# Feed-forward entry on Trainium2: seven of eight sums of quarters of the normalised rows on GpSimd instead of VectorE

## The chip, the cores and the metric

The kernel runs on one core of a Trainium2 chip. A core has TensorE (matrix products and transposes, results in PSUM), VectorE, ScalarE and GpSimd (elementwise work, each with an instruction queue of its own that it executes in order) and SyncE, which here issues all DMAs. The metric is the device time of one execution in microseconds (us). Before the change it was 2821.42 us, the median of three runs (2820.86 to 2824.37).

## The reference

A trunk of two layers over 512 tokens of width 1024. Each layer has four sublayers, each between two RMS norms and added to the running state `h`: a feed-forward block, a mixer (a gated delta rule in the first layer, a state-space scan in the second), a cross attention over 256 memory rows, and another feed-forward block. So there are four feed-forward blocks, and they are what the change touches:

```python
def swiglu(x, w_in, w_out):
    gate, up = jnp.split(x @ w_in, 2, axis=-1)
    return (jax.nn.silu(gate) * up) @ w_out

u = swiglu(rms_norm(h, g[0, 0]), ffn_w_in[l, 0], ffn_w_out[l, 0])
h = h + MACARON_W * rms_norm(u, g[0, 1])
```

`x` is 512 x 1024, `w_in` 1024 x 5632, `w_out` 2816 x 1024, all in float32.

## The kernel before

Every float32 product is made of three products in a reduced format: each operand is split into a high part (a cast, by ScalarE) and a low part (the difference, by VectorE), and high x high, high x low and low x high are added up in PSUM (`mm3`, L144 to L146).

The feed-forward block computes gate and up with a scheme after Strassen and Winograd: the 512 x 1024 input is cut in four quarters, A11 and A21 being the left half of the columns of tokens 0 to 255 and 256 to 511, A12 and A22 the right half. Seven products of quarters and of sums of quarters replace eight. The sums needed are S1 = A21 + A22, S2 = S1 - A11, S3 = A11 - A21 and S4 = A12 - S2.

The tokens come in four tiles of 128. `FFN.enter(i, ss, tag)` (L367) takes tile i of the state, normalises it on VectorE (L374, two halves of 512 columns: `u <- h, rcol, pg`), and for each quarter or sum calls `put`: four transposes on TensorE into one PSUM bank (L380), the high part by ScalarE (L382), the low part by VectorE (L383). Tiles 0 and 1 give A11 and A12. Tiles 2 and 3 ("third" and "fourth") give A22, S1, S2, S4 and S3; the sums are formed with the rows of tile i - 2, in place, by four instructions of 128 x 512: s1 (L392), S3's operand (L394), S2's operand (L395), S4's operand (L397). Each but the second needs the one before it or s1, and S2's operand needs s1, S4's operand needs S2's.

Entry is not a stage of its own. `run` calls for each tile i the last output products of the sublayer before (`tail`), then `post` (the norm behind that sublayer, L226 and L231 on VectorE), then `enter`. With the fourth tile `head(0)` begins: the weights of the first two pairs are loaded and split (L130, L131), and products of A11 and A12 alone are formed (`early`), which need nothing of tiles 2 and 3. After that comes `plain`, which forms a difference of raw weights (L455) and splits it (`split`, L138 and L139), and later `pair` (L474).

The order of the instructions on each engine is not written by hand: a scheduler places them by priority (`later` shifts it) and by its own estimate of how long each takes. So a change of engine for one instruction moves others, too. PSUM tiles `ps_c` (the transposes) have two banks, the tile `xs` (s1) two buffers.

Of the kernel before, what the change touches and what calls it, by code (L numbers as in the profile page):

```python
# [14 lines left out]
ALU = mybir.AluOpType  # L15
# [38 lines left out]
def prio(name):  # L54
    def wrap(f):
        def g(self, *a, **k):
            with getattr(self, "t", self).later(name):
                return f(self, *a, **k)
        return g
    return wrap  # L60
# [275 lines left out]
class FFN:  # L336
# [29 lines left out]
    @prio('ff_enter')  # L366
    def enter(self, i, ss, tag):  # L367

        t, nc = self.t, self.t.nc
        r = t.rcol(ss)  # L370
        x = t.u[:, i, :]
        a, b = slice(0, T), slice(T, D)
        for s in (a, b):
            nc.vector.scalar_tensor_tensor(x[:, s], t.h[:, i, s], r[:, 0:1], self.pg[:, s], op0=ALU.mult, op1=ALU.mult)  # L374
        ts = slice(i % 2 * P, i % 2 * P + P)

        def put(src, dst):
            ps = t.bank(tag)
            for k in range(4):
                nc.tensor.transpose(ps[:, k * P:k * P + P], src[:, k * P:k * P + P], t.cst(C_ID))  # L380
            p = ps.rearrange("p (k t) -> p k t", k=4)
            nc.scalar.copy(dst[0][:, :, ts], p)  # L382
            nc.vector.tensor_sub(dst[1][:, :, ts], p, dst[0][:, :, ts])  # L383

        if i < 2:
            put(x[:, a], self.A11)
            put(x[:, b], self.A12)
        else:
            y = t.u[:, i - 2, :]
            put(x[:, b], self.A22)  # L390
            s1 = t.nt.tile([P, T], F32, name="xs", bufs=2)
            nc.vector.tensor_add(s1, x[:, a], x[:, b])  # L392
            put(s1, self.S1)
            nc.vector.tensor_sub(x[:, a], y[:, a], x[:, a])  # L394
            nc.vector.tensor_sub(y[:, a], s1, y[:, a])  # L395
            put(y[:, a], self.S2)
            nc.vector.tensor_sub(y[:, b], y[:, b], y[:, a])  # L397
            put(y[:, b], self.S4)
            put(x[:, a], self.S3)

# [921 lines left out]
def run(t, phases, n0=0):  # L1322
# [17 lines left out]
    with ExitStack() as c:  # L1340
        if hasattr(phases[0], "gains"):
            phases[0].gains(c, n0)
            phases[0].sums()
        for i in range(NT):
            if i:
                t.load(i)
            ss = t.nt.tile([P, 2], F32, name="ssh", bufs=2)
            for f in range(2):
                t.sumsq(t.h[:, i, f * T:f * T + T], ss[:, f:f + 1], f and i < 2)
            enter(i, n0, phases[0], ss, "cscc"[i])  # L1350
            if i % 2:
                phases[0].head(i // 2, i == 1)
        t.load_rest()
    for j, ph in enumerate(phases):
        n = n0 + j
        nxt = phases[j + 1] if j + 1 < len(phases) else None
        with ExitStack() as c:
            if hasattr(nxt, "gains"):
                nxt.gains(c, n + 1)
            ph.open(c)  # L1360
            t.post_gain(n)
            t.warm(AF.Silu, t.xh[:, KB - 1, T - 1:T])
            ph.rest()
            if hasattr(nxt, "sums"):
                nxt.sums()
            for i in range(NT):
                t.tail(ph, i)
                if i == 0:
                    t.warm(AF.Sqrt, t.ssu[:, 0, 0:1])
                if i == NT - 1:  # L1370
                    c.close()
                    if nxt:
                        nxt.head(0)
                ss = t.post(i, nxt)
                if nxt:
                    enter(i, n + 1, nxt, ss)
                else:
                    for f in range(2):
                        fs = slice(f * T, f * T + T)
                        nc.sync.dma_start(out=t.ap["out"][i * P:(i + 1) * P, fs], in_=t.h[:, i, fs])  # L1380
            if nxt:
                nxt.head(1)
# [41 lines left out]
```

## Time and profile before

| | |
|---|---|
| median of three runs | 2821.42 us |
| the profiled execution | 2822.96 us |
| its span | 2821.2 us |
| TensorE busy | 2771.5 us (98%) |
| VectorE busy | 2078.6 us (74%) |
| ScalarE busy | 1509.3 us (53%) |
| GpSimd busy | 129.4 us (5%) |
| mean granted TensorE clock | 0.998 |

The span is the time from the first to the last instruction of the profiled execution; that execution was 1.54 us longer than the median. Shares are means over the whole span. In the rows below DVE is VectorE, ACT ScalarE, POOL GpSimd, PE TensorE; "L392" is line 392 of the kernel. A row of the timeline has the start, the time taken, the engine, the line, the operation, output<-inputs, the count, and in brackets how long the engine had been idle before and for what it had waited.

### The profile page before, as it was taken

How to read it: one execution, taken by the hardware profiler on the slowest of the kernel's cores; microseconds unless marked ns; L12 is line 12 of the kernel's file. 1: busy time of each engine (PE TensorE's matmuls, PEld its weight loads, DVE VectorE, ACT ScalarE, POOL GpSimd, SP SyncE). 2: the span in 40 equal slices, each digit the busy share in tenths (PEclk: the TensorE clock that was granted, in tenths of full speed). 3: DMA queues.
4: the chain of work that ended last, by engine and by line, in shares of the span. 5: the costliest groups of instructions: out<-in, count | busy, mean ns of one | idle time of the engine just before them, and what ended most of it. 6: DMA issues, size and time to landing. Idle time of an engine off the chain costs nothing.

```text
span 2821.2 us, 45001 instructions
## 1 busy us (share of the span) xinstructions
PE 2771.5 (98%) x17328; PEld 2451.3 (87%) x17328; DVE 2078.6 (74%) x4057; ACT 1509.3 (53%) x2760; POOL 129.4 (5%) x141
## 2 busy tenths in 40 slices
PE   8999999999999999999999999999999999999998
PEld 7999987888887887999988999888888888799997
DVE  8887777767667565887778877777667766588776
ACT  5444486766475574544355444575554656454433
POOL 0000001100000000000000000013212200000000
PEclk9999999999999999999999999999999999999999
DMA  6333534233324532332343332433233363133233
GB/s 217 106 105 103 159 124 119 77 115 86 100 71 138 189 113 79 121 113 90 112 150 128 98 105 96 147 121 112 83 105 110 100 223 112 69 112 113 96 107 105
DMA packets 144758, 326.51 MB, mean 116 GB/s; under 512 B 36080, under 2 KB 65520, under 8 KB 144032
## 3 DMA queue, kind: packets, MB, share of 16 engines
q1 hardware_dynamic: 144544, 323.63, 35.3%
q8 instruction: 137, 2.24, 0.3%
q14 instruction: 77, 0.63, 0.1%
HBM read 297.27 MB, written 26.31 MB: 115 GB/s over the span
## 4 chain that ended last, share of the span: by engine, by line
PE 84%; DVE 7%; ACT 4%; DMA 3%; issue 1%; POOL 0%; SPq 0%; DVEq 0%; ACTq 0%; POOLq 0%
PE ps_a L144 16%; PE ps_a L145 16%; PE ps_a L146 16%; PE ps_s L145 5%; PE ps_s L146 4%; PE ps_s L144 4%; PE ps_c L144 2%; PE ps_c L146 2%; PE ps_c L145 2%; PE ps_f L145 2%; PE ps_f L146 2%; PE ps_f L144 2%; DVE wlo L131 1%; PE ps_c L1060 1%; PE ps_s L1229 1%
## 5 line engine op out<-in xcount | busy, mean ns | idle before, releaser
L144 PE MATMUL ps_a<-xh,whi 128*128 128x256 f32 (+1 forms) x2368 | 751.7, 320 | 2.8 <-ACT z L871 1.6
L145 PE MATMUL ps_a<-xl,whi 128*128 128x256 f32 (+1 forms) x2368 | 748.9, 318 | 0.3 <-DVE xl L383 0.3
L146 PE MATMUL ps_a<-xh,wlo 128*128 128x256 f32 (+1 forms) x2368 | 746.4, 317 | 0.0
L144 PEld LDWEIGHTS ps_a<-xh,whi 128*128 128x128 f32 x2368 | 452.0, 191 | 31.6 <-ACT xh L382 2.0
L145 PEld LDWEIGHTS ps_a<-xl,whi 128*128 128x128 f32 x2368 | 452.9, 191 | 26.6 <-DVE xl L383 0.7
L146 PEld LDWEIGHTS ps_a<-xh,wlo 128*128 128x128 f32 x2368 | 452.9, 191 | 23.9
L131 DVE TENSOR_TENSOR wlo<-raw,whi 128x1024 fp32r<-128x1024 f32 x278 | 340.7, 1228 | 172.6 <-ACT whi L130 170.6
L130 ACT CAST whi<-raw 128x1024 fp32r<-128x1024 f32 x278 | 289.6, 1043 | 219.6 <-PE ps_a L145 122.8
L138 ACT CAST whi<-h 128x1024 fp32r<-128x1024 f32 x168 | 175.6, 1048 | 203.2 <-PE ps_a L145 149.8
L139 DVE TENSOR_TENSOR wlo<-h,whi 128x1024 fp32r<-128x1024 f32 x168 | 205.3, 1224 | 89.1 <-ACT whi L138 88.5
L493 ACT CAST bh<-raw 128x512 fp32r<-128x512 f32 x80 | 49.7, 621 | 167.6 <-DMA raw<-ffn_in 135.7
L145 PE MATMUL ps_s<-wlo,hhi 128*128 128x512 f32 x352 | 138.0, 392 | 0.0
L144 PE MATMUL ps_s<-whi,hhi 128*128 128x512 f32 x352 | 137.8, 392 | 0.0
L146 PE MATMUL ps_s<-whi,hlo 128*128 128x512 f32 x352 | 137.2, 390 | 0.0
L146 PE MATMUL ps_c<-whi,hlo 128*128 128x512 f32 x288 | 112.0, 389 | 0.0
L144 PE MATMUL ps_c<-whi,hhi 128*128 128x512 f32 x288 | 112.0, 389 | 0.0
L145 PE MATMUL ps_c<-wlo,hhi 128*128 128x512 f32 x288 | 112.0, 389 | 0.0
L138 ACT CAST whi<-raw 128x1024 fp32r<-128x1024 f32 x80 | 84.0, 1050 | 51.0 <-PE ps_c L146 39.4
L486 DVE TENSOR_TENSOR h<-raw 128x512 f32<-128x512 f32 x80 | 55.1, 689 | 70.7 <-DMA raw<-ffn_in 67.5
L139 DVE TENSOR_TENSOR wlo<-raw,whi 128x1024 fp32r<-128x1024 f32 x80 | 97.5, 1219 | 9.0 <-ACT whi L138 9.0
L513 ACT ACTIVATE h<-h 128x512 f32<-128x512 f32 x80 | 50.6, 633 | 83.8 <-DVE h L510 83.6
L469 ACT CAST hhi<-h 128x512 fp32r<-128x512 f32 x88 | 54.8, 622 | 72.1 <-DVE h L514 43.1
(418 smaller groups left out, 6620.3 us busy)
## 6 DMA issues: line engine op xcount, KB each, us to landing
raw<-ffn_in SPq DMA_DIRECT2D x192, 512.0 KB, 4.2
raw<-ffn_out SPq DMA_DIRECT2D x88, 512.0 KB, 3.5
raw<-dn_in SPq DMA_DIRECT2D x48, 512.0 KB, 3.5
raw<-ssd_in SPq DMA_DIRECT2D x32, 512.0 KB, 3.6
hd<-h SPq DMA_DIRECT2D x24, 512.0 KB, 3.2
h<-hd SPq DMA_DIRECT2D x24, 512.0 KB, 4.3
raw<-dn_out SPq DMA_DIRECT2D x16, 512.0 KB, 3.8
raw<-xa_k SPq DMA_DIRECT2D x16, 512.0 KB, 4.3
```

The source lines that it names most:

```text
L130: nc.scalar.copy(hi[:, :n], raw[:, :n])
L131: nc.vector.tensor_sub(lo[:, :n], raw[:, :n], hi[:, :n])
L138: nc.scalar.copy(hi, raw)
L139: nc.vector.tensor_sub(lo, raw, hi)
L144: mm(ps, lhs[0], rhs[0], start=first, stop=False)
L145: mm(ps, lhs[0], rhs[1], start=False, stop=False)
L146: mm(ps, lhs[1], rhs[0], start=False, stop=last)
L469: self.t.nc.scalar.copy(hi, x)
L486: sub(T1, u[:, a], g[:, a])
L493: nc.scalar.copy(b22[0], u[:, b])
L513: nc.scalar.activation(gt, gt, AF.Silu)
L1060: nc.tensor.matmul(py[:, e * 64:e * 64 + 64], st["gp"][e][:, c, :], st["xt"][:, c, e * 64:e * 64 + 64], start=True, stop=True)
```

## The change

In `enter`, for the third tile all four sums are formed by GpSimd, for the fourth tile the last three; the first sum of the fourth tile (s1) stays on VectorE. That is seven instructions in each of the four entries. Nothing else is edited; what is computed is the same.

```diff
             put(x[:, b], self.A22)
             s1 = t.nt.tile([P, T], F32, name="xs", bufs=2)
-            nc.vector.tensor_add(s1, x[:, a], x[:, b])
+            op = nc.gpsimd.tensor_tensor
+            if i == 2:
+                op(s1, x[:, a], x[:, b], op=ALU.add)
+            else:
+                nc.vector.tensor_add(s1, x[:, a], x[:, b])
             put(s1, self.S1)
-            nc.vector.tensor_sub(x[:, a], y[:, a], x[:, a])
-            nc.vector.tensor_sub(y[:, a], s1, y[:, a])
+            op(x[:, a], y[:, a], x[:, a], op=ALU.subtract)
+            op(y[:, a], s1, y[:, a], op=ALU.subtract)
             put(y[:, a], self.S2)
-            nc.vector.tensor_sub(y[:, b], y[:, b], y[:, a])
+            op(y[:, b], y[:, b], y[:, a], op=ALU.subtract)
             put(y[:, b], self.S4)
             put(x[:, a], self.S3)
```

Lines behind the edit have numbers that are higher by four in the changed kernel (L455 is L459, for example).

TensorE in the fourth entry, third tile, before: from the transposes of A22 (`u`) and of S1 (`xs`) on; behind the last row shown 14 more products stand before the transposes of S2.

```order
L380 MATMUL ps_c<-const,u 128x128 [waits DVE_49,PE_49]
L380 MATMUL ps_c<-const,u 128x128 x3
L144 MATMUL ps_s<-thi,xh 128x512
L380 MATMUL ps_c<-const,xs 128x128 [waits DVE_49,PE_49]
L380 MATMUL ps_c<-const,xs 128x128 x3
L145 MATMUL ps_s<-tlo,xh 128x512
```

The same place in the changed kernel, down to the transposes of S2 (the last `u`).

```order
L380 MATMUL ps_c<-const,u 128x128 [waits DVE_49,PE_49]
L380 MATMUL ps_c<-const,u 128x128 x3
L144 MATMUL ps_s<-thi,xh 128x512
L380 MATMUL ps_c<-const,xs 128x128 [waits PE_49,Pool_49]
L380 MATMUL ps_c<-const,xs 128x128 x3
L145 MATMUL ps_s<-tlo,xh 128x512
L146 MATMUL ps_s<-thi,xl 128x512
L144 MATMUL ps_a<-xh,whi 128x256
L145 MATMUL ps_a<-xl,whi 128x256
L146 MATMUL ps_a<-xh,wlo 128x256
L380 MATMUL ps_c<-const,u 128x128 [waits DVE_49,Pool_49]
```

Five products stand between the transposes of S1 and those of S2 where there were 15, and both now wait for GpSimd (Pool).

VectorE at the same place before, from the second half of L374 of the third tile to its low part of S2.

```order
L374 SCALAR_TENSOR_TENSOR u<-h,rcol,pg 128x512
L392 TENSOR_TENSOR xs<-u 128x512 [waits DVE_49]
L455 TENSOR_TENSOR h<-raw 128x512 [waits DMAHW0_49]
L394 TENSOR_TENSOR u<-u 128x512 [waits DVE_49]
L383 TENSOR_TENSOR xl<-ps_c,xh 128x4x128 [waits Activation_49]
L395 TENSOR_TENSOR u<-xs,u 128x512 [waits DVE_49]
L383 TENSOR_TENSOR xl<-ps_c,xh 128x4x128 [waits Activation_49]
L397 TENSOR_TENSOR u<-u 128x512 [waits DVE_49]
L226 TENSOR_TENSOR u<-u,gbc 128x512 [waits Activation_49]
L383 TENSOR_TENSOR s2l<-ps_c,s2h 128x4x128 [waits Activation_49]
```

And in the changed kernel, down to the low part of S3.

```order
L374 SCALAR_TENSOR_TENSOR u<-h,rcol,pg 128x512
L459 TENSOR_TENSOR h<-raw 128x512 [waits DMAHW0_49]
L383 TENSOR_TENSOR xl<-ps_c,xh 128x4x128 [waits Activation_49]
L139 TENSOR_TENSOR wlo<-h,whi 128x1024 [waits Activation_49]
L383 TENSOR_TENSOR xl<-ps_c,xh 128x4x128 [waits Activation_49]
L383 TENSOR_TENSOR s2l<-ps_c,s2h 128x4x128 [waits Activation_49]
L226 TENSOR_TENSOR u<-u,gbc 128x512 [waits Activation_49]
L203 TENSOR_TENSOR rcol<-ssu 128x1
L383 TENSOR_TENSOR s4l<-ps_c,s4h 128x4x128 [waits Activation_49]
L459 TENSOR_TENSOR h<-raw 128x512 [waits DMAHW1_49,DVE_49]
L383 TENSOR_TENSOR s3l<-ps_c,s3h 128x4x128 [waits Activation_49]
```

The four sums are gone from VectorE's queue, the split L139 has moved ahead of the low part of S1, and the low parts of S2, S4 and S3 stand ahead of the norm of the next tile (L231, three rows further on) as before.

TensorE in the third entry, third tile, in the changed kernel: the transposes of S1 follow those of A22 directly, where six products stood between them.

```order
L380 MATMUL ps_c<-const,u 128x128 [waits DVE_49,PE_49]
L380 MATMUL ps_c<-const,u 128x128 x3
L380 MATMUL ps_c<-const,xs 128x128 [waits PE_49,Pool_49]
L380 MATMUL ps_c<-const,xs 128x128 x3
L145 MATMUL ps_a<-xl,whi 128x256
```

Behind them 17 products follow before the transposes of S2, where there were 22.

## Rows read from the trace of the kernel before

**Rows 1.** Busy time, share and instructions by engine, from the page.

```profile
PE 2771.5 (98%) x17328; PEld 2451.3 (87%) x17328; DVE 2078.6 (74%) x4057; ACT 1509.3 (53%) x2760; POOL 129.4 (5%) x141
```

**Rows 2.** Waits of PE: who for whom, us in total, times, longest.

```profile
PE ps_c L380 <- DVE u L374: 13.5, 8, 7.8
```

**Rows 3.** Windows: busy per engine, PEclk, DMA share and GB/s, third entry.

```profile
1490.00:1495.00 5.00, 1.62 (x14) 1.43 (x13) 4.97 (x10) 1.84 (x6) 0.00 (x0) 1.00 0.68 246
...
1496.20:1503.00 6.80, 5.70 (x27) 5.17 (x27) 5.02 (x9) 3.91 (x8) 0.00 (x0) 0.52 0.16 60
```

**Rows 4.** One moved line's durations (min/median/max), and the group of L1044.

```profile
L394 DVE TENSOR_TENSOR u<-u x8: 678/688/692, 24.4 to 2476.3; 128x512 f32<-128x512 f32 x8
...
L1044 POOL TENSOR_TENSOR gp<-gp,di 128x512 f32<-128x512 f32 x32 | 47.2, 1475 | 123.1 <-DVE gp L1040 97.6 <-DVE rsy L313 13.1 <-ACT sjunk L1104 6.2
```

**Rows 5.** Timeline of GpSimd, 1899 to 1905 us.

```profile
1899.53 1.29 POOL L1044 TENSOR_TENSOR gp<-gp,di 128x512 f32<-128x512 f32 x1 [17.51 <-DVE gp L1040]
1900.91 0.60 POOL L1043 TENSOR_SCALAR di<-const,rows 128x128 f32<-128x128 f32 x1
1901.48 3.71 POOL L1044 TENSOR_TENSOR gp<-gp,di 128x512 f32<-128x512 f32 x1
```

**Rows 6.** Timeline of VectorE beside it.

```profile
1901.34 2.70 DVE L1036 SCALAR_TENSOR_TENSOR gp<-gp,sA,const 128x128 f32<-128x128 f32 x10
```

**Rows 7.** Timeline of VectorE: alone, beside GpSimd with PSUM, beside GpSimd with SBUF.

```profile
1929.85 1.22 DVE L1100 TENSOR_TENSOR y<-y,sz 128x1024 f32<-128x1024 f32 x1
...
1945.69 0.73 DVE L1117 SCALAR_TENSOR_TENSOR solo<-ps_c,sng,sohi 128x512 fp32r<-128x512 f32 x1
...
1967.13 1.94 DVE L1100 TENSOR_TENSOR y<-y,sz 128x1024 f32<-128x1024 f32 x1
```

**Rows 8.** Timeline of GpSimd at the second and third of these.

```profile
1945.62 1.29 POOL L1044 TENSOR_TENSOR gp<-gp,di 128x512 f32<-128x512 f32 x1
...
1966.70 1.28 POOL L1044 TENSOR_TENSOR gp<-gp,di 128x512 f32<-128x512 f32 x1 [4.41 <-DVE gp L1040]
```

**Rows 9.** Timeline of VectorE, fourth entry.

```profile
2459.95 1.40 DVE L374 SCALAR_TENSOR_TENSOR u<-h,rcol,pg 128x512 f32<-128x512 f32 x2
...
2462.99 0.69 DVE L455 TENSOR_TENSOR h<-raw 128x512 f32<-128x512 f32 x1 [0.91 <-DMA raw<-ffn_in]
...
2470.57 1.40 DVE L231 SCALAR_TENSOR_TENSOR h<-u,rcol,h 128x512 f32<-128x512 f32 x2
...
2474.16 1.42 DVE L374 SCALAR_TENSOR_TENSOR u<-h,rcol,pg 128x512 f32<-128x512 f32 x2
```

**Rows 10.** Timeline of TensorE, fourth entry: S1 of tile three, S3 of tile four.

```profile
2462.23 0.63 PE L380 MATMUL ps_c<-const,xs 128*128 128x128 f32 x4
...
2480.89 0.60 PE L380 MATMUL ps_c<-const,u 128*128 128x128 f32 x4
```

**Rows 11.** Timeline of ScalarE, fourth entry: the cast of the raw difference.

```profile
2463.72 1.05 ACT L138 CAST whi<-h 128x1024 fp32r<-128x1024 f32 x1 [0.96 <-DVE h L455]
```

**Rows 12.** Timeline of VectorE, second entry.

```profile
1125.01 0.69 DVE L455 TENSOR_TENSOR h<-raw 128x512 f32<-128x512 f32 x1
```

**Rows 13.** Timeline of VectorE, third entry.

```profile
1479.82 1.40 DVE L374 SCALAR_TENSOR_TENSOR u<-h,rcol,pg 128x512 f32<-128x512 f32 x2
1481.15 0.68 DVE L226 TENSOR_TENSOR u<-u,gbc 128x512 f32<-128x512 f32 x1
...
1485.42 1.21 DVE L131 TENSOR_TENSOR wlo<-raw,whi 128x1024 fp32r<-128x1024 f32 x1
```

**Rows 14.** Timeline of TensorE, third entry: A22 and S3 of tile four.

```profile
1495.01 0.63 PE L380 MATMUL ps_c<-const,u 128*128 128x128 f32 x4 [3.40 <-DVE u L374]
...
1502.98 0.60 PE L380 MATMUL ps_c<-const,u 128*128 128x128 f32 x4
```

**Rows 15.** Timeline of VectorE, first entry.

```profile
20.98 1.22 DVE L131 TENSOR_TENSOR wlo<-raw,whi 128x1024 fp32r<-128x1024 f32 x1
```

## The prediction

> **What bounds the kernel now.** I read the busy shares first: TensorE is busy for 98% of the span [rows 1]. So a saving elsewhere counts only where TensorE stands still, and a new stop of TensorE counts in full. The list of who waited for whom comes second: TensorE's largest wait is that of the transposes (L380) for the normalised rows (L374), 13.5 us in eight places, 7.8 us of it in one, at the start, where the first rows have to be loaded [rows 2]. The places are the feed-forward entries, of which there are four: at about 10 to 40, 1105 to 1150, 1465 to 1505 and 2440 to 2487 us. Third, the windows around the third entry: TensorE is busy for 1.62 of 5 us there, and behind that gap its granted clock averages 0.52 over 6.8 us, which is the lower of its levels, 1.2 GHz instead of 2.4 [rows 3]. That stretch loses (1 - 0.52) x 6.8 = 3.3 us. Fourth, the timelines of VectorE, GpSimd and TensorE inside the entries, from which the terms come.
>
> **What is moved.** Each entry forms four sums per tile (S1's operand s1, then those of S3, S2, S4) for the third and the fourth tile. Seven of the eight go from VectorE to GpSimd: 28 instructions in all. On VectorE one took 0.69 us [rows 4]. No plain add or subtraction of this shape runs on GpSimd before; the nearest is the addition at L1044, 128x512 in float32, 1.475 us on the mean [rows 4] and 1.29 us when nothing holds it, with the next GpSimd instruction 1.38 us behind its start [rows 5]. I take 1.29 us and 1.38 us from step to step. The low bound is VectorE's own 0.69, the high one the 3.71 us below.
>
> **What the two engines do to each other.** The second L1044 in rows 5 took 3.71 us. Beside it VectorE ran ten instructions in a row with two operands in SBUF (gp and a constant), 2.70 us of them from 1901.34 on [rows 6]; the addition ends 1.2 us after their end (1904.0), so it did its work only then. It goes the other way too: the product at L1100 takes 1.22 us alone and 1.94 us when it is issued while a GpSimd addition runs [rows 7, 8]: 0.72 us more. Against VectorE instructions that read PSUM there is no such effect: L1117 keeps its 0.73 us beside an addition that keeps its 1.29 us [rows 7, 8]. In an entry most of VectorE's work has two SBUF operands (L226, L231, L374, L131, L139, the differences of raw weights). Only the five low parts per tile (L383) read PSUM, and GpSimd can have these 0.6 us each to itself. So a moved sum frees 0.6 us on VectorE and blocks it for up to 0.7 us (1.29 less one L383 beside it). VectorE gains about nothing, and the chain s1, S3's, S2's, S4's grows from 4 x 0.6 to 4 x 1.38 us at least.
>
> The Trainium skill, page "SBUF — State Buffer", section "SBUF: two separate sides", calls this an exclusive lock: whichever of the two starts first keeps it for its whole instruction. The trace agrees on the 0.72 us. But by the page GpSimd would get its turn when one instruction ends, where the 3.71 us show that ten passed first. What the milder reading would give is the second rival.
>
> **TensorE's order.** It executes in order, and in the new order the transposes of S2 stand 5 matrix products behind those of S1 instead of 15 (third tile of the second and fourth entry), and in the third entry the transposes of S1 follow those of A22 with none between. They were placed as if a sum were ready sooner than 1.38 us after the one before.
>
> **Fourth entry, step by step.** L374 ends at 2461.36, and the next VectorE instruction, the raw difference, waits for its transfer until 2462.99 [rows 9]. So s1 runs at once, 2461.45 to 2462.75, and the transposes of S1 start at 2462.85, not 2462.23 [rows 10]: 0.6 us. S3's operand follows at 2462.83 to 2464.13; the raw difference is held and then goes first (to 2464.75); S2's operand: 2464.75 to 2466.05. TensorE has done its 5 products at about 2464.15 and waits 2.0 us. S4's operand must let L139 pass (1.2 us; its input, the cast L138 of 1.05 us [rows 11], is late as well): 2467.2 to 2468.5. TensorE, 13 products later, waits 0.5 us. On VectorE the low parts of S2 and S4 and ScalarE's square root for the last tile stand behind these transposes, so L231 moves from 2470.57 to about 2472.3 and L374 of the fourth tile, 3.6 us behind it [rows 9] and now also behind a cast of 0.6 us, from 2474.16 to 2476.5. There three sums of 1.38 us follow the second L374 and s1: S4's operand is ready at 2482.7, the last transposes start at about 2483.5 instead of 2480.89 [rows 10]. The 44 products behind them are the same. Term: 2.6 us.
>
> **Second entry.** The order is the same, but the raw difference finds its data at 1125.01 [rows 12], less than 1 us behind L374's end. Then L139 is ready when S3's operand ends and, if it wins, goes before S2's: 1.2 us more, 3.9 us; without that 2.7. I take the middle, 3.3.
>
> **Third entry.** Behind L374 (to 1481.2) VectorE now has L226 twice and L131 back to back [rows 13]. If s1 is kept out as in rows 5, it starts at 1481.2 + 0.6 + 0.6 + 0.1 + 1.1 = 1483.6 and ends at 1484.9; TensorE, done with A22's transposes at 1481.9, waits 3.1 us. The fourth tile comes about 1.5 us late, where TensorE had waited 3.40 us [rows 14]; that wait shrinks to about 0.5, two new ones of about 2 and 1 us follow. The last transposes start at about 1501.8 instead of 1502.98 [rows 14], but with 44 products (0.12 us each) behind them instead of 34: 0 in sum if the clock stays up, 3.3 us if it falls for as long as before. Term: 1.5 us, between these.
>
> **First entry.** L131 from 20.98 on [rows 15] keeps s1 out, TensorE's order is as tight as in the others, and GpSimd's first sum may start slowly. I did not count it through: the mean of the second and fourth, 3.0 us, between 0 (TensorE is still waiting for loads) and 6.
>
> Sum: 3.0 + 3.3 + 1.5 + 2.6 = 10.4 us. The profiled execution took 2822.96 us, 1.54 us above the median of 2821.42. So 2833.4 for an execution like that one, and **2832 us** by the median. Nothing takes it back later: inside the feed-forward stages TensorE is the engine that is waited for.
>
> **Rivals.** First, a gain: the third entry's stop goes. VectorE has seven sums less ahead of L374 of the fourth tile there; were GpSimd's sums not in its way, 4 us of VectorE's time would come free, the wait of 3.40 us would vanish and with it the slow clock's 3.3 us. It decides if L374's wait there falls below 1 us and no other wait in that entry is over 1 us. Price: -6.7 us there and up to -1 us, TensorE's smaller waits, in each of the three others: 2812. For it: the wait is for VectorE [rows 14]. Against it: VectorE is not freed while GpSimd holds it up, and S1's transposes stand directly behind A22's. Second, the mild form: GpSimd gets in after any one VectorE instruction. Then the second entry costs 2.7, the third 1.8 less wait for s1 (about -1, its clock staying up), the fourth 2.0, the first 1: about 5 us, 2826. Third, the hard form: stops of 2 to 3 us lower the clock in two of the other entries too, 3.3 us each as in rows 3, and the chains are kept out longer: 10.4 + 6.6 + 2 = 19 us, 2840. For it: the clock fell once behind a stop of 3.40 us. Against it: the new stops are shorter. A change that does nothing would have to hide all 28 sums behind TensorE's products; the new order has too few of them in between.
>
> **How the numbers follow.** Forecast 0.52, the mild form 0.22, the hard form 0.14, the gain 0.12. Over 0.2% is over 5.6 us, about what can be told from no change here. Slower (forecast and hard form): 0.66. Within 0.2% (the mild form): 0.22. Faster: 0.12, at most. The range takes in the forecast, the mild form and the hard form but for its far end, and leaves most of the gain out: 2818 to 2844. Around the forecast alone it is 2827 to 2838.
>
> **What would show it.** In the changed profile: the 28 sums on GpSimd with a mean of about 1.5 to 2 us; VectorE's L374, L226 or L139 stretched to 1.2 us and more beside them; new waits of TensorE's L380 for GpSimd, about 2 to 3 us in each entry; in the third, one of 3 us for s1 in place of the 3.40 us for L374. It is wrong if TensorE's waits for GpSimd come to less than 4 us in all, or if VectorE's stretched instructions don't appear. If the granted clock stays at its upper level through the third entry, only that entry's term is wrong, by 1.5 us.

## The result and the profile after

The changed kernel takes 2842.5 us (median of 6 runs, 2839.58 to 2843.88); the kernel before took 2823.92 (median of 6, the three given further up among them). The ratio is 1.0065, 95% interval 1.0055 to 1.0075: 18.6 us slower. 2832 had been forecast, in a range of 2818 to 2844. The profiled execution took 2840.85 us with a span of 2838.8.

The page's row of busy times after the change:

```profile
PE 2775.0 (98%) x17328; PEld 2454.6 (86%) x17328; DVE 2067.2 (73%) x4029; ACT 1508.3 (53%) x2760; POOL 173.6 (6%) x169
```

Against [rows 1], VectorE has 28 instructions fewer and is busy for 11.4 us less, GpSimd for 44.2 us more. TensorE's waits at the transposes, after (who for whom, us in total, times, longest):

```profile
PE ps_c L380 <- POOL u L399: 13.0, 8, 2.5
PE ps_c L380 <- DVE u L374: 12.1, 7, 8.3
PE ps_s L380 <- DVE u L374: 4.8, 1, 4.8
...
PE ps_c L380 <- POOL xs L394: 4.2, 4, 1.6
PE ps_c L380 <- POOL u L401: 2.5, 6, 0.9
```

The wait for VectorE's L374 of [rows 2] is little changed; 19.7 us of waits for GpSimd are new, 13.0 of them for S2's operand (L399), which stands third in the chain s1, S3's, S2's, S4's. Some waits for VectorE have shrunk: all of TensorE's waits at L380 together have grown from 20.3 to 36.6 us, by 16.3. The four groups of sums on GpSimd (busy us, mean ns of one):

```profile
L399 POOL TENSOR_TENSOR u<-xs,u 128x512 f32<-128x512 f32 x8 | 12.3, 1542 | 0.6
L398 POOL TENSOR_TENSOR u<-u 128x512 f32<-128x512 f32 x8 | 11.9, 1492 | 39.7 <-PE ps_c L380 32.5 <-DVE xs L396 6.9
L401 POOL TENSOR_TENSOR u<-u 128x512 f32<-128x512 f32 x8 | 11.9, 1484 | 0.6
L394 POOL TENSOR_TENSOR xs<-u 128x512 f32<-128x512 f32 x4 | 7.0, 1746 | 820.4 <-DMA raw<-ffn_in 460.5 <-DVE u L374 339.3 <-DVE rcol L203 20.7
```

28 sums in 43.1 us, where 28 undisturbed ones of 1.28 would take 35.8: GpSimd was itself kept waiting for 7.3 us. The second entry shows how. GpSimd, third tile:

```profile
1131.45 1.27 POOL L394 TENSOR_TENSOR xs<-u 128x512 f32<-128x512 f32 x1 [261.79 <-DMA raw<-ffn_in]
1132.80 1.62 POOL L398 TENSOR_TENSOR u<-u 128x512 f32<-128x512 f32 x1
1134.50 2.24 POOL L399 TENSOR_TENSOR u<-xs,u 128x512 f32<-128x512 f32 x1
```

VectorE beside it:

```profile
1132.16 1.10 DVE L459 TENSOR_TENSOR h<-raw 128x512 f32<-128x512 f32 x1 [0.94 <-DMA raw<-ffn_in]
...
1134.39 1.23 DVE L139 TENSOR_TENSOR wlo<-h,whi 128x1024 fp32r<-128x1024 f32 x1 [0.52 <-ACT whi L138]
```

TensorE's transposes of S1 and S2:

```profile
1132.78 0.66 PE L380 MATMUL ps_c<-const,xs 128*128 128x128 f32 x4 [0.54 <-POOL xs L394]
1136.79 0.66 PE L380 MATMUL ps_c<-const,u 128*128 128x128 f32 x4 [2.53 <-POOL u L399]
```

The raw difference L459 (0.69 alone [rows 12]) is held to 1.10 by the first sum; the second sum is held in turn; the third loses its turn to L139 by 0.11 us and takes 2.24. TensorE has five products between the two groups and stands still for 2.53 us.

Windows of the changed kernel in which the granted clock is low (columns as in [rows 3]; the last three are PEclk, DMA share, GB/s):

```profile
28.50:32.50 4.00, 4.00 (x23) 4.00 (x23) 2.24 (x3) 1.04 (x2) 0.00 (x0) 0.58 0.17 46
459.00:466.00 7.00, 6.18 (x27) 5.26 (x26) 3.47 (x13) 3.98 (x7) 0.64 (x1) 0.54 0.63 200
1138.20:1141.80 3.60, 3.60 (x21) 3.60 (x21) 1.74 (x4) 1.18 (x4) 0.00 (x0) 0.58 0.37 108
1513.60:1517.20 3.60, 3.56 (x19) 3.56 (x20) 1.62 (x4) 1.69 (x3) 1.27 (x1) 0.57 0.02 5
```

The third entry keeps a stretch at 1.2 GHz, about half as long as in [rows 3]; the first and second have one of that length each, and the gated delta rule of the first layer ("DeltaNet" below) a longer one. In the kernel before, the first two entries have none:

```profile
28.00:33.00 5.00, 4.98 (x43) 4.78 (x42) 4.87 (x8) 4.10 (x6) 0.00 (x0) 1.00 0.33 116
1120.00:1145.00 25.00, 24.06 (x178) 22.06 (x177) 23.57 (x41) 14.91 (x31) 0.00 (x0) 1.00 0.60 216
```

**Where the time went.** The table gives how much later than in the kernel before the work is, split by place. Each figure is the difference of two starts of VectorE's reciprocal (L205), at 355.84, 1094.88, 1462.28, 1821.12, 2432.09 and 2811.18 us of the kernel before; each is from one profiled execution. An entry's column takes in its whole feed-forward block; DeltaNet and SSD (the state-space scan) take in the cross attention behind them. The experiments below are in it already.

| kernel | entry 1 | DeltaNet | entry 2 | entry 3 | SSD | entry 4 | sum |
|---|---|---|---|---|---|---|---|
| changed kernel | 5.9 | 1.2 | 5.3 | 2.5 | -0.4 | 3.2 | 17.7 |
| idle additions beside the sums | 3.4 | -0.2 | 4.0 | 3.9 | 1.1 | 3.5 | 15.7 |
| the same, half as wide | 2.4 | 0.1 | 2.3 | 0.9 | -0.4 | 1.1 | 6.4 |
| the same, outside the entries | -0.4 | -2.6 | 1.3 | 0.6 | 0.3 | 0.1 | -0.7 |
| sums on GpSimd, order of before | 4.3 | 2.2 | 3.4 | 1.4 | 0.4 | 3.0 | 14.8 |
| sums on VectorE, order of the change | 4.7 | 0.9 | 1.3 | -0.7 | 0.2 | 0.7 | 7.2 |
| S3's operand alone on GpSimd | 1.5 | -0.6 | 4.8 | 2.4 | -1.2 | 5.1 | 12.0 |
| all but S3's operand | 3.5 | 2.4 | 3.0 | 1.0 | 1.3 | 1.8 | 13.1 |
| first entry alone | 6.7 | 1.3 | 1.1 | -0.4 | 0.1 | -0.1 | 8.8 |
| fourth tile alone | 4.7 | -1.3 | 1.5 | 1.5 | 0.2 | 0.5 | 7.1 |

Where a kernel changes nothing in a place, the place still differs by up to 1.3 us, DeltaNet by more; finer figures than that are not read from it.

### The profile page after: what moved, and what is told of

It is laid out like the page before. It is cut to its first block, busy times and chain, and to the rows that moved or that the text cites. A ratio compares the mean times of both kernels' runs of the same rounds, so it can differ in the third digit from the quotient of the medians.

```text
span 2838.8 us, 45035 instructions
## 1 busy us (share of the span) xinstructions
PE 2775.0 (98%) x17328; PEld 2454.6 (86%) x17328; DVE 2067.2 (73%) x4029; ACT 1508.3 (53%) x2760; POOL 173.6 (6%) x169
## 3 DMA queue, kind: packets, MB, share of 16 engines
q8 instruction: 137, 2.24, 0.3%
## 4 chain that ended last, share of the span: by engine, by line
PE 83%; DVE 7%; ACT 4%; DMA 3%; issue 2%; POOL 1%; POOLq 0%; SPq 0%; DVEq 0%; ACTq 0%
PE ps_a L144 15%; PE ps_a L145 15%; PE ps_a L146 15%; PE ps_s L145 4%; PE ps_s L146 4%; PE ps_s L144 4%; PE ps_c L146 2%; PE ps_c L144 2%; PE ps_c L145 2%; PE ps_f L145 2%; PE ps_f L146 2%; PE ps_f L144 2%; DVE wlo L131 1%; PE ps_c L1064 1%; PE ps_s L773 1%
## 5 line engine op out<-in xcount | busy, mean ns | idle before, releaser
L131 DVE TENSOR_TENSOR wlo<-raw,whi 128x1024 fp32r<-128x1024 f32 x278 | 339.7, 1224 | 169.3 <-ACT whi L130 167.4
L139 DVE TENSOR_TENSOR wlo<-h,whi 128x1024 fp32r<-128x1024 f32 x168 | 205.4, 1224 | 91.1 <-ACT whi L138 90.1
L139 DVE TENSOR_TENSOR wlo<-raw,whi 128x1024 fp32r<-128x1024 f32 x80 | 97.5, 1219 | 9.6 <-ACT whi L138 9.6
```

Source lines behind the costliest of these rows:

```text
L131: nc.vector.tensor_sub(lo[:, :n], raw[:, :n], hi[:, :n])
L139: nc.vector.tensor_sub(lo, raw, hi)
```

## The experiments

The theories: A, the chain of sums on GpSimd (1.38 us a step) is what TensorE waits for; B, the two engines' sharing of SBUF is the price, whoever forms the sums; C, TensorE's new order of instructions is the price. After the first four runs A and B became S: the engines take turns, and both the sums and VectorE's other work come late. The experiments were measured in three groups, each beside its own runs of the kernel before, so the time that they are compared with differs by up to 0.5 us.

**Idle additions beside the sums.** The kernel before, with

```diff
+            rep = t.nt.tile([P, T], F32, name="xs", bufs=2)
+            for _ in range(6 - i):
+                nc.gpsimd.tensor_tensor(rep, x[:, b], x[:, b], op=ALU.add)
             put(s1, self.S1)
```

> The sums stay on VectorE, and GpSimd makes seven additions of the same size per entry beside them (28 in all) into a tile that nobody reads; TensorE's order in the second, third and fourth entry is that of the kernel before. Theory A (the cost of the change is the chain of sums itself: 1.38 us a step on GpSimd and turns lost to VectorE, in front of transposes for which TensorE stops): nothing waits for GpSimd here, VectorE alone is held by up to 0.7 us at a time, so +2 to +5 us over the kernel before, 2826 to 2829. Theory B (the price is the sharing of SBUF: VectorE is held up by whatever GpSimd does): +15 to +19 us, 2839 to 2843, as with the change. Theory C (the price is the new order of TensorE's transposes): 0 to +3 us, 2824 to 2827, and the whole of it in the first entry, whose order differs.

Measured: 2838.95 against 2822.74 us, ratio 1.0063 (1.0051 to 1.0076). Theory B's number, and a miss for A as I had priced it. GpSimd in the fourth entry:

```profile
2473.76 5.74 POOL L395 TENSOR_TENSOR xs<-u 128x512 f32<-128x512 f32 x4 [198.88 <-DVE u L374]
2489.55 4.46 POOL L395 TENSOR_TENSOR xs<-u 128x512 f32<-128x512 f32 x3 [10.05 <-DVE u L374]
```

VectorE beside it (L392, L397, L398, L400 are the sums):

```profile
2473.58 0.69 DVE L392 TENSOR_TENSOR xs<-u 128x512 f32<-128x512 f32 x1
2474.72 0.99 DVE L458 TENSOR_TENSOR h<-raw 128x512 f32<-128x512 f32 x1 [0.45 <-DMA raw<-ffn_in]
2475.64 1.52 DVE L397 TENSOR_TENSOR u<-u 128x512 f32<-128x512 f32 x1
2477.09 0.68 DVE L383 TENSOR_TENSOR xl<-ps_c,xh 128x512 fp32r<-128x512 f32 x1
2477.69 0.92 DVE L398 TENSOR_TENSOR u<-xs,u 128x512 f32<-128x512 f32 x1
2478.53 0.68 DVE L383 TENSOR_TENSOR xl<-ps_c,xh 128x512 fp32r<-128x512 f32 x1
2479.13 0.92 DVE L400 TENSOR_TENSOR u<-u 128x512 f32<-128x512 f32 x1
```

Each sum that meets an addition takes 0.92 to 1.52 us instead of 0.69 [rows 4]; the low parts L383, which read PSUM, keep their 0.68 and let the next addition pass. In this entry seven VectorE instructions are longer than their like in the kernel before, by 3.45 us in all, and the entry is 3.5 us late. In the second and third the same count gives 3.5 and 4.0, the delays are 4.0 and 3.9. So in these three entries, in which the order of TensorE, VectorE and ScalarE is that of before, the block is late by what VectorE is held up in it, close to one for one; in the third a longer low clock has a part (0.50 over 10.2 us from 1503.8 on, 3.4 us longer than before). The first entry is no such case: TensorE's order there is another.

**The same, half as wide.**

```diff
-                nc.gpsimd.tensor_tensor(rep, x[:, b], x[:, b], op=ALU.add)
+                nc.gpsimd.tensor_tensor(rep[:, 0:256], x[:, b][:, 0:256], x[:, b][:, 0:256], op=ALU.add)
```

> As the run with 28 additions beside the sums, with half of the columns in each (128x256). TensorE's order in the second to fourth entry is that of before. Theory S (turns on SBUF, each costing what is left of GpSimd's instruction): GpSimd's additions take about 0.65 us, so half of what 28 whole ones cost (+16 us): +6 to +9 us, 2829 to 2832. Rival (a fixed price for each GpSimd instruction, or for its start, whatever its size): +14 to +16 us, 2837 to 2839.

Measured: 2828.5 against 2822.24 us, ratio 1.0023 (1.0014 to 1.0032): +6.3 us, in the range of S. The additions take 0.61 us at the least and 1.11 on the mean (31.0 us for 28), since they too wait for turns, and VectorE is held up for 4.9 us in the four entries, where the whole ones held it for 14.4. The price falls with that, though not one for one in every entry; a fixed price per instruction is out.

**The same, outside the entries.** In the block of products (`pair`), for n = 6 and 8:

```diff
         sub(T3, u[:, b], u[:, a])
+        if n in (6, 8):
+            rep = t.nt.tile([P, T], F32, name="xs", bufs=2)
+            for _ in range(7 - n // 2):
+                nc.gpsimd.tensor_tensor(rep, T4, T1, op=ALU.add)
```

> All sums on VectorE; the same 28 additions of 128x512 on GpSimd as in the first run with additions beside the sums, seven per feed-forward stage, but put beside the differences of raw weights of two later blocks of each stage (n = 6 and 8) instead of the entry. Theory S, narrowed (VectorE's held time counts only where TensorE stands right behind VectorE's chain, in the entries): 0 to +2 us over the kernel before, 2822 to 2824. Rival (GpSimd's share of SBUF costs TensorE wherever it is taken): +13 to +16 us, 2835 to 2839.

Measured: 2822.16 against 2822.41 us, ratio 0.9999 (0.999 to 1.0008). The page's row:

```profile
PE 2770.0 (98%) x17328; PEld 2451.7 (87%) x17328; DVE 2091.4 (74%) x4057; ACT 1507.0 (53%) x2760; POOL 181.5 (6%) x169
```

VectorE is held up here too, by 2091.4 - 2078.6 = 12.8 us, for nothing. Time taken from VectorE cost something in the entries, where TensorE stands right behind it, and nothing at this place.

**Order and engine apart.** Two kernels in which TensorE's instructions of the four entries are held to a given order by edges that set the issue order and add no wait:

```diff
+    for c in ORDER:
+        names = ["I-%d" % k for a, b in c for k in range(a, b + 1)]
+        for p, q in zip(names, names[1:]):
+            tc.add_manual_dep(by[q], p, info, reason="order")
```

First the changed kernel in the order of before.

> The changed kernel (28 sums on GpSimd), but TensorE's instructions of the four entries are held to the order of the kernel before (15 products between the transposes of S1 and S2 in the second and fourth entry instead of 5, and so on); issue order alone, no added wait. Theory C (the order makes the price): back to +0 to +4 us over the kernel before, 2823 to 2827. Theory S (the two engines take turns on SBUF, so that the sums come at 1.3 to 1.4 us a step and VectorE's other work is late, whatever the order): the wider order hides at most 10 products of 0.12 us per wait, some 8 us in all, so +10 to +14 us, 2833 to 2837.

Measured: 2835.73 against 2822.24 us, ratio 1.0049 (1.0036 to 1.0061): +13.5 us, as S had it. Its largest waits of TensorE at the transposes:

```profile
PE ps_c L380 <- DVE u L374: 11.7, 7, 8.2
...
PE ps_c L380 <- POOL u L399: 5.4, 7, 1.4
```

Then the kernel before in the order of the change.

> The kernel before (all sums on VectorE, at 0.69 us), but TensorE's instructions of the four entries are held to the order of the changed kernel. Theory C (the order makes the price): as the change, +15 to +19 us, 2838 to 2842. Theory S (turns on SBUF): the sums come at VectorE's pace and TensorE waits at most 0.6 us at some of the eight groups: 0 to +4 us, 2823 to 2827. If both theories carry a part, this and the run with the wide order on GpSimd add up to about 18 us.

Measured: 2829.38 against 2822.24 us, ratio 1.002 (1.001 to 1.003): +7.1 us by the medians, 5.6 by the ratio. Neither theory's range holds; what holds is the last sentence, that both carry a part.

```profile
PE ps_c L380 <- DVE u L374: 11.5, 6, 8.7
PE ps_c L380 <- DVE u L395: 6.7, 5, 1.7
```

The wider order brings the waits for S2's operand from 13.0 to 5.4 us, and the closer order makes 6.7 us of them even at VectorE's pace. 13.5 and 7.1 add up to 20.6 beside the 18.6 of both together: roughly two thirds of the price go with the sums on GpSimd, one third with TensorE's order. This is not a clean split: only TensorE's order was held, the scheduler moved some of VectorE's instructions in both kernels too, and the two parts need not add up. By place they differ: in entries 2 to 4 the order alone costs 1.3 us in sum and GpSimd alone 7.8; in the first either costs 4 to 5, and both together 5.9.

**Parts of the change.** Only S3's operand on GpSimd:

```diff
-            nc.vector.tensor_sub(x[:, a], y[:, a], x[:, a])
+            nc.gpsimd.tensor_tensor(x[:, a], y[:, a], x[:, a], op=ALU.subtract)
```

> Only the operand of S3 is formed on GpSimd (8 sums of 28); it is the one that no other sum needs and that is transposed last. Theory A (the chain): TensorE waits less than 1 us in all for GpSimd; VectorE's own chain loses about 0.6 us per tile where a sum lies beside it: +2 to +5 us, 2826 to 2829. Theory B (sharing of SBUF): 8/28 of the measured 18.6 us, +5 us, 2829. Theory C (the order): TensorE's order is nearly as tight as with the change (in the fourth tile of three entries no product between the transposes of S1 and S2), so +12 to +18 us, 2836 to 2842.

Measured: 2834.17 against 2822.74 us, ratio 1.0041 (1.0028 to 1.0055): +11.4 us for 8 sums, above A and B and just below C. VectorE and then TensorE, fourth tile of the fourth entry:

```profile
2485.05 0.69 DVE L392 TENSOR_TENSOR xs<-u 128x512 f32<-128x512 f32 x1
2487.18 0.69 DVE L395 TENSOR_TENSOR u<-xs,u 128x512 f32<-128x512 f32 x1 [1.44 <-POOL u L394]
```

```profile
2485.88 0.63 PE L380 MATMUL ps_c<-const,xs 128*128 128x128 f32 x4
2488.53 1.12 PE L380 MATMUL ps_c<-const,u 128*128 128x128 f32 x4 [2.02 <-DVE xl L383]
```

My expectation was wrong in a plain way: S2's operand is written over the half that S3's operand reads (`y[:, a]`), so S3's sum stands in the chain (the dependences listed with the kernel before leave this one out), and VectorE waits 1.44 us for it. S2's transposes stand right behind S1's here, and TensorE waits 2.02 us. That is not the whole price. The clock is at its lower level in three stretches of the entries (columns as in [rows 3]):

```profile
1146.20:1149.80 3.60, 3.53 (x19) 3.41 (x17) 1.88 (x4) 1.45 (x3) 0.00 (x0) 0.53 0.00 0
1501.00:1511.60 10.60, 8.28 (x37) 7.41 (x38) 7.47 (x12) 4.99 (x9) 1.26 (x1) 0.52 0.31 101
2487.60:2494.60 7.00, 6.07 (x29) 6.08 (x30) 4.15 (x7) 2.77 (x7) 0.00 (x0) 0.51 0.01 2
```

Worked out as in the prediction, they lose 1.7, 5.1 and 3.4 us, where the kernel before loses 3.3 in its one stretch: 6.9 us more, against 12.0 that this execution is late.

The rest of the chain on GpSimd, S3's operand on VectorE:

```diff
-            op(x[:, a], y[:, a], x[:, a], op=ALU.subtract)
+            nc.vector.tensor_sub(x[:, a], y[:, a], x[:, a])
```

> S3's operand goes back to VectorE; S1's (third tile), S2's and S4's stay on GpSimd (20 sums of 28). TensorE's order is that of the change almost everywhere. Theory A (the chain): S2's operand no longer stands behind S3's, one step of 1.38 us less per tile; TensorE's wait for S2's operand, 13.0 us with the change, falls to about 4 to 6, so 7 to 10 us less than the change: +8 to +12 us over the kernel before, 2832 to 2836. Theory B (sharing): 20/28 of 18.6, +13 us, 2837. Theory C (the order): as the change, +17 to +19 us, 2841 to 2843.

Measured: 2832.94 against 2822.74 us, ratio 1.0038 (1.0026 to 1.0051): +10.2 us, in A's range, and TensorE's wait for S2's operand fell as A had it:

```profile
PE ps_c L380 <- POOL u L399: 5.3, 6, 1.4
```

Two parts of 8 and 20 sums cost 11.4 and 10.2, together more than the whole: the price is not one per sum, and the clock has a share in it that changes from version to version.

The first entry alone, and (the second line) the fourth tile's three sums alone:

```diff
-            op = nc.gpsimd.tensor_tensor
+            op = nc.gpsimd.tensor_tensor if self.idx == 0 else nc.vector.tensor_tensor
...
+            op = nc.gpsimd.tensor_tensor if i == 3 else nc.vector.tensor_tensor
```

> The change in the first of the four entries alone (7 sums of 28). Theory A (each entry pays for itself and nothing takes it back): the 5.9 us that the changed kernel was late behind its first entry, give or take what the next stage adds: +5 to +7 us, 2827 to 2829. Rival (the first entry's delay is given back where later stages wait for loads): 0 to +2 us, 2822 to 2824.

> Only the fourth tile's three sums per entry are formed on GpSimd (12 of 28). Theory A (the end of an entry is set by the fourth tile's chain, in which three steps cost 0.7 us more each): about 2 us per entry, +6 to +9 us, 2828 to 2831. Rival (the price is made by the third tile's four sums, which hold up the VectorE work that the fourth tile's rows wait for): +1 to +4 us, 2823 to 2826.

Measured: 2828.79 against 2822.41 us, ratio 1.0024 (1.0014 to 1.0033), and 2830.28 against the same, ratio 1.0024 (1.0015 to 1.0034). The first entry's delay stays to the end. The fourth tile has about 7 us of the 18.6; theory A's range holds, but 4.7 us of the table's 7.1 are in the first entry and only 0.5 to 1.5 in each of the others, not 2 in each.

**Two attempts without GpSimd.** The four sums on VectorE ahead of its other work, and the transposes of the sums behind other products; here one of four lines each:

```diff
+            with t.later("ff_sum"):      # ff_sum=-100
+                nc.vector.tensor_add(s1, x[:, a], x[:, b])
...
+            with t.later("ff_sum"):      # ff_sum=100
+                put(s1, self.S1)
```

> No GpSimd: the four sums stay on VectorE, with a higher priority than its other work, so that in the first and third entry TensorE's transposes stand about as close as with the change, and the second and fourth entries keep TensorE's order of before. Theory A (the chain): a step is 0.69 us, so the close order can be kept up with: -3 to +1 us, 2821 to 2825. Theory B (sharing): 0. Theory C (the order): the first and third entry cost about what they cost with the change, 5.9 and 2.5 us: +6 to +9 us, 2830 to 2833.

> The kernel before, no GpSimd; the transposes of the four sums get a lower priority, so that in all entries those of S3 of the fourth tile stand some 60 products later. If the price of all these versions is TensorE's waits for VectorE's chain in the entries, moving a transposition that nothing needs yet out of the way takes off its small waits there (1 to 2 us in each of three entries): -1 to -4 us, 2819 to 2822. If these waits are the chain itself, which the last transposes do not shorten: 0, 2823. A rival with a loss: the products that need S3 come late, +2 to +5 us.

Measured: 2826.36 against 2822.74 us, ratio 1.0017 (1.0008 to 1.0025), and 2828.8 against 2822.24 us, ratio 1.0024 (1.0013 to 1.0034). The first lies between the theories. For the second, the rival with a loss was nearest; its 8.4 us in the trace lie in the first entry (3.3) and DeltaNet (4.4), and in DeltaNet the granted clock averages 0.50 over 10.3 us from 456.3 on, where the kernel before has no such stretch; whether that is the whole of the 4.4 us is not shown. Neither beats the kernel before, and no other version here does.

## Why the prediction was right, and where its sizes were off

**The mechanism** is as predicted: the engines hold each other up, a sum on GpSimd starts 1.35 us after the one before where nothing holds it (1132.80 less 1131.45; 1.38 had been taken), TensorE's order leaves too few products, and nothing is given back later. Most of the signs came: the 28 sums have a mean of 1.54 us, TensorE waits 19.7 us for GpSimd, and two L374 in the first entry take 2.97 us (from 25.35 on), where two take 1.40 in [rows 9]. A stretched L139 could not have been one, since 1.2 us is what it takes alone.

**The size was not.** 2842.5 us lies outside the 2827 to 2838 that had been given for the forecast alone. It is near the 2840 of the hard form, which had a chance of 0.14, and it lies in the stated range because that had been drawn wide enough to take the hard form in. That part is luck; the direction and the cause are not.

**The turns on SBUF: half right.** From [rows 5, 6] I had GpSimd kept out by whole rows of VectorE instructions, and in the third entry by L226 twice, L203 and L131, 3.7 us from L374's end to the end of s1. There it was kept out by the two L226 and then got in ahead of L203 and L131: s1 took 2.20 us (both rows stand in the last section). No sum took over 2.28 us. But the reading of [rows 5] was no accident of one place. The same addition takes as long in the changed kernel, again beside ten VectorE instructions:

```profile
1916.04 3.71 POOL L1048 TENSOR_TENSOR gp<-gp,di 128x512 f32<-128x512 f32 x1
```

In the run with idle additions one of them in the third entry takes 2.56 us, beside L226, L392 and L226 in a row (1488.35 to 1490.24):

```profile
1488.58 2.56 POOL L395 TENSOR_TENSOR xs<-u 128x512 f32<-128x512 f32 x1 [340.98 <-DVE u L374]
```

The prediction quoted the Trainium skill, page "SBUF — State Buffer", section "SBUF: two separate sides", for an exclusive lock held for one whole instruction; the changed kernel's rows agree with that (2.24 us beside the 1.23 of L139). After how many VectorE instructions GpSimd gets in differs in these rows, and what decides it is open. Most of the sums that were held met only one VectorE instruction with two operands in SBUF, so the mild form's premise was seldom put to the test; its price of 5 us was far off all the same, because the sums and VectorE's work come late together even so.

**"VectorE gains about nothing"** was too gloomy as a sum (it was busy for 11.4 us less) and beside the point: the chain is slower whoever is less busy.

**Fourth entry, 2.6 predicted, 3.2 found.** The waits of the third tile came about as worked out: S1's 0.54 us (0.6), S2's 1.57 (2.0), S4's 0.16 (0.5). The last transposes:

```profile
2497.80 0.66 PE L380 MATMUL ps_c<-const,u 128*128 128x128 f32 x4 [0.23 <-POOL u L401]
2498.53 0.62 PE L380 MATMUL ps_c<-const,u 128*128 128x128 f32 x4
```

2498.53 less the 14.5 us that this kernel was late before the entry is 2484.0; 2483.5 had been predicted, 2480.89 stood in [rows 10].

**Second entry, 3.3 predicted, 5.3 found.** L139 did go first, which I had priced at 3.9 and averaged away. The rest is the clock: the window 1138.20 to 1141.80 above loses (1 - 0.58) x 3.6 = 1.5 us. That belonged to the hard form.

**Third entry, 1.5 predicted, 2.5 found.** S1's wait:

```profile
1496.02 0.66 PE L380 MATMUL ps_c<-const,xs 128*128 128x128 f32 x4 [1.52 <-POOL xs L394]
...
1509.89 0.63 PE L380 MATMUL ps_c<-const,u 128*128 128x128 f32 x4 [1.79 <-DVE u L374]
...
1513.64 1.12 PE L380 MATMUL ps_c<-const,u 128*128 128x128 f32 x4 [2.39 <-POOL u L399]
```

1.52 us, not 3.1; L374's wait fell from 3.40 [rows 14] to 1.79, not 0.5; and S2's in the fourth tile is 2.39. The clock fell for half as long as before. TensorE's waits in this block rose by 3.1 us (4.5 to 7.6) and the clock lost 1.5 where it had lost 3.3: that accounts for 1.3 of the 2.5 us; the rest I did not find.

**First entry, 3.0 predicted, 5.9 found: the term that failed.** It was set at the mean of two others and not counted through. Counted now: TensorE waits 5.5 us there for GpSimd, and the window 28.50 to 32.50 loses 1.7, together 1.3 more than the entry was late. The close order costs 4.7 us in this entry even with VectorE's sums, 1.7 of them by a low clock there as well (0.66 over 36 to 41 us). It was the only entry whose order I did not count through.

**The sum.** 10.4 became 17.7 in the profiled execution: 2.9 more in the first entry, 2.0 in the second, 1.0 in the third, 0.6 in the fourth and 0.8 between them, which is within what unchanged places differ by. Of the hard form two lower clocks in other entries came true, shorter than it had them (1.5 and 1.7 us, not 3.3 each); its chains that were kept out longer did not.

## What to carry to other kernels

Before work moves from VectorE to GpSimd, look at what stands beside it. Where the bounding engine waited right behind VectorE, GpSimd instructions with SBUF operands cost about what they held VectorE up, even though nobody needed their output; elsewhere 12.8 us of the same were free. A scheduler may place dependent groups closer together in the bounding engine's order than the work between them takes, so compare that order and count the products between two dependent groups. And an entry that looks like the others should still be counted through: the term set by analogy was the one most wrong.

## What the runs showed that had not been expected

A VectorE instruction on one column was held as long as a large one. Third entry of the changed kernel, VectorE:

```profile
1490.88 0.16 DVE L203 TENSOR_TENSOR rcol<-ssh 128x1 f32<-128x1 f32 x1
...
1493.54 1.28 DVE L226 TENSOR_TENSOR u<-u,gbc 128x512 f32<-128x512 f32 x2
1494.75 1.24 DVE L203 TENSOR_TENSOR rcol<-ssu 128x1 f32<-128x1 f32 x1
```

GpSimd beside L226 and the second L203:

```profile
1493.77 2.20 POOL L394 TENSOR_TENSOR xs<-u 128x512 f32<-128x512 f32 x1 [339.27 <-DVE u L374]
```

The same stop of TensorE in DeltaNet leaves the clock up in one kernel and is followed by the lower level in another. Before and after the change:

```profile
449.00:453.00 4.00, 1.74 (x9) 0.98 (x9) 3.83 (x12) 3.97 (x8) 0.00 (x0) 1.00 0.63 130
453.00:460.00 7.00, 5.56 (x43) 4.86 (x42) 5.33 (x16) 4.79 (x9) 0.90 (x1) 1.00 0.66 208
```

```profile
455.00:459.00 4.00, 1.75 (x8) 1.00 (x7) 3.83 (x12) 3.97 (x8) 0.00 (x0) 0.94 0.65 142
```

Behind the second comes the window 459 to 466 shown above, at 0.54. The stop is the same to 0.01 us; what decided is open. So a time difference of a few microseconds in DeltaNet is not put down to the change.
